# A fixed order for the seven products of the up projection, and weights of two early pairs made earlier

## The chip, the cores and the metric

The kernel runs on one core of one Trainium2 chip. The metric is device time in microseconds. The core has five engines with queues of their own that run in order: TensorE (PE, matmuls into PSUM), VectorE (DVE), ScalarE (ACT), GpSimd (POOL) and SyncE (SP, which issues most transfers).

## The reference

One layer of a decoder trunk over 1,024 tokens of width 1,024, in fp32: three mixers and an output projection, cross-attention over 256 memory tokens, and a gated MLP, each with a residual, and an RMSNorm at the end. The change lies at the end of the cross-attention and in the MLP:

```python
x = x + memory_cross_attention(h, rms_norm(mem, norm_mem_g[l]), ...)
h = rms_norm(x, norm_ffn_g[l])
x = x + conv_gated_ffn(h, ffn_w_up[l], ffn_conv_w[l], ffn_conv_b[l], ffn_w_down[l])
...
def conv_gated_ffn(h, w_up, conv_w, conv_b, w_down):
    u, v = jnp.split(h @ w_up, 2, axis=-1)
    u = lax.conv_general_dilated(u, conv_w[:, None, :], ...) + conv_b   # causal, width 3
    return (jax.nn.silu(u) * v) @ w_down
```

The hidden width of u and of v is 22 blocks of 128.

## The kernel before

Every fp32 product is made of three matmuls on rounded parts: each operand is split into a high part (`hi`, a ScalarE copy) and the rest (`lo`, a subtraction on VectorE or GpSimd), and hi x hi, hi x lo and lo x hi are summed in PSUM.

**Last attention product.** `tokmajor` multiplies the softmax by the prepared value weights (`vo_dram`), for two halves of tokens (0 to 3, 4 to 7, in blocks of 128) and two halves of columns, with four weight pieces each. A piece is loaded by SP (L137) into one of two `raw` buffers, cast to `whi` by ScalarE (L140), and `wlo` is made on VectorE (L143). `last` takes each finished block: residual sum (L1263), store of x2 (L1266, SP), norm (L1112 to L1115), and then the operands of the MLP, transposed on TensorE (L1254) and split (L1257, L1258).

**Up projection.** u and v of one block of hidden columns (a pair) are made with seven products in place of eight, as in Strassen's scheme over two halves of tokens and two halves of depth. The token operands are B11, B21 (tokens 0 to 3), T1, T2, T4 and later T3, B22 (with tokens 4 to 7). The weight operands are blocks of the raw weights (`t_up`) or sums of them made on GpSimd (`left`, L1308), each split into a `wf` tile (L1315 ScalarE, L1316 VectorE and GpSimd in turn). Each of the seven is twelve matmuls of 128x512 (`prod`, L1323). Raw weights lie in the two `raw` buffers and in residual rows that have come free. `ahead(f)` makes the B11 and B21 products of the first six pairs early and stores them in DRAM; `pair(f)` makes the others, for 22 pairs. Products go to PSUM tiles `ps_a` (B11, then B21), `ps_b2` (T2) and `ps_cd`, one tile of two halves c and d:

```python
cd = self.dps.tile([P, 1024], F32, tag="d", name="ps_cd")
c, d = cd[:, 0:512], cd[:, 512:1024]
...
self.prod(c, next(forms), X["T3"], True, True)
V.tensor_tensor(out=u3, in0=c, in1=u2, op=ALU.add)
self.prod(d, next(forms), X["T1"], True, True)
V.tensor_tensor(out=vt[:, 512:1024], in0=d, in1=u3, op=ALU.add)
```

T4 then adds to c and B22 to d, each read once more by VectorE (L1392, L1394). ScalarE and VectorE make the convolution and the gate from u (`y`, L1396 to L1400), and y goes to DRAM.

**Down projection.** `ffn_down` loads y and the weights again, splits both (`wd`, L1446 and L1447; `ap`, L1449 and L1450) and sums over 22 blocks in eight PSUM banks (`ps_dn`, L1436).

**Order.** The program is written in the order of the code; a scheduler then orders the instructions of each engine by its own estimate of times, and puts in the waits between engines. So products of neighbouring pairs are interleaved on TensorE.

Of the kernel before, what the change touches and what calls it, by code (L numbers as in the profile page):

```python
# [12 lines left out]
F32 = mybir.dt.float32  # L13
# [4 lines left out]
ALU = mybir.AluOpType  # L18
# [3 lines left out]
P = 128  # L22
S = 1024
DM = 1024
NK = 8
# [71 lines left out]
class K:  # L97
# [1098 lines left out]
    def trunk(self, mT, qk_dram, vo_dram, x2_dram, bp):  # L1196

        nc, tc, I = self.nc, self.tc, self.I
        V, A, G, T = nc.vector, nc.scalar, nc.gpsimd, nc.tensor

        xr = []
        for i in range(8):
            xr.append(self.res.tile([P, DM], F32, tag=f"r{i}", name="xr"))
            nc.sync.dma_start(out=xr[i], in_=I["x"][0, P * i:P * i + P, :])

        def resid(nm, g, T2):
            def f(c, i, o):
                xs = xr[i][:, 512 * c:512 * c + 512]
                V.tensor_tensor(out=xs, in0=o, in1=xs, op=ALU.add)
                if c == 1:  # L1210
                    xn = bp.tile([P, DM], F32, tag="xn", name="xn", bufs=2)
                    self.norm_g(bp, xr[i], g, xn)
                    self.to_T(xn, T2, i)
            return f

        h2 = self.halves("h2T")
        g2 = self.gain(bp, I["norm_xa_g"])
        self.tokmajor(I["t_out"], mT, resid("xa", g2, h2))
        pT = self.halves("pT")

        def soft(c, i, o):

            nm, z = (self.tiny.tile([P, 2], F32, tag=t, name=t, bufs=3) for t in ("s_nm", "s_z"))
            V.tensor_reduce(out=nm, in_=o.rearrange("p (h n) -> p h n", n=256), op=ALU.max, axis=AX.X)
            G.tensor_scalar(out=nm, in0=nm, scalar1=-1.0, scalar2=None, op0=ALU.mult)
            p_ = bp.tile([P, DM], F32, tag="xn", name="s_p", bufs=2)
            for j in range(2):
                js = slice(256 * j, 256 * j + 256)
                A.activation(out=p_[:, js], in_=o[:, js], func=AF.Exp, bias=nm[:, j:j + 1], accum_out=z[:, j:j + 1])
            V.reciprocal(out=z, in_=z)  # L1230
            ps = self.mps.tile([P, 512], F32, tag="m", name="ps_pT")
            for j in range(2):
                js = slice(256 * j, 256 * j + 256)
                G.tensor_scalar(out=p_[:, js], in0=p_[:, js], scalar1=z[:, j:j + 1], scalar2=None, op0=ALU.mult)
                for n in (2 * j, 2 * j + 1):
                    T.transpose(ps[:, P * n:P * n + P], p_[:, P * n:P * n + P], self.ident)
            p3 = ps.rearrange("p (k t) -> p k t", t=P)
            ts = slice(P * (i % 4), P * (i % 4) + P)
            hi, lo = (blk(pT[a][i // 4], c)[:, :, ts] for a in range(2))
            A.copy(out=hi, in_=p3)  # L1240
            V.tensor_tensor(out=lo, in0=p3, in1=hi.bitcast(F32), op=ALU.subtract)

        self.tokmajor(qk_dram, h2, soft)
        g3 = self.gain(bp, I["norm_ffn_g"])
        X, xk, held = {}, [], []

        def form(n, x, i):

            if n not in X:
                X[n] = [self.quad(f"{n}{p}") for p in ("hi", "lo")]  # L1250
            ts = slice(P * (i % 4), P * (i % 4) + P)
            ps = self.mps.tile([P, 512], F32, tag="m", name="ps_T")
            for j in range(4):
                T.transpose(ps[:, P * j:P * j + P], x[:, P * j:P * j + P], self.ident)  # L1254
            p3 = ps.rearrange("p (k t) -> p k t", t=P)
            hi, lo = (x[:, :, ts] for x in X[n])
            A.copy(out=hi, in_=p3)  # L1257
            V.tensor_tensor(out=lo, in0=p3, in1=hi.bitcast(F32), op=ALU.subtract)  # L1258

        def last(c, i, o):  # L1260

            xs = xr[i][:, 512 * c:512 * c + 512]
            V.tensor_tensor(out=xs, in0=o, in1=xs, op=ALU.add)  # L1263
            if c == 0:
                return
            nc.sync.dma_start(out=x2_dram[i], in_=xr[i])  # L1266
            if i % 2 == 0 and i < 4:
                xk.append(self.quad("xk", F32, (P, 2, DM)))
            xn = xk[i // 2][:, i % 2, :] if i < 4 else self.res.tile([P, DM], F32, tag=f"r{i - 4}", name="xn")
            self.norm_g(bp, xr[i], g3, xn)  # L1270
            x1, x2 = xn[:, 0:512], xn[:, 512:1024]
            if i < 4:
                form("B11", x1, i)
                form("B21", x2, i)
                return
            k = xk[i // 2 - 2]
            t1, t4 = k[:, i % 2, 0:512], k[:, i % 2, 512:1024]
            t2 = bp.tile([P, DM], F32, tag="xn", name="t2", bufs=2)[:, 0:512]
            V.tensor_tensor(out=t1, in0=x1, in1=t1, op=ALU.subtract)
            V.tensor_tensor(out=t2, in0=x2, in1=t1, op=ALU.subtract)  # L1280
            G.tensor_tensor(out=t4, in0=t4, in1=t2, op=ALU.subtract)
            G.tensor_tensor(out=x1, in0=x2, in1=x1, op=ALU.subtract)
            for n, x in (("T2", t2), ("T1", t1), ("T4", t4)):
                form(n, x, i)
            held.append((i, x1, x2))

        self.tokmajor(vo_dram, pT, last)
        for n in range(2):
            for i, *x in held:
                form(("T3", "B22")[n], x[n], i)  # L1290
        return X

    def left(self, r1, r2, which, sp):

        nc = self.nc
        V, A, G = nc.vector, nc.scalar, nc.gpsimd
        q = {f"A{n}{k + 1}": r[:, 4 * k:4 * k + 4, :] for n, r in ((1, r1), (2, r2)) if r is not None for k in range(2)}
        sums = {"S1": ("A21", "A22", ALU.add), "S2": ("S1", "A11", ALU.subtract), "S3": ("A11", "A21", ALU.subtract),  # L1300
                "S4": ("A12", "S2", ALU.subtract)}

        def get(n):
            if n not in q:
                a, b, op = sums[n]
                a, b = get(a), get(b)
                q[n] = sp.tile([P, 4, P], F32, tag=n, name=n, bufs=2 if n in ("S1", "S2") else 1)
                G.tensor_tensor(out=q[n], in0=a, in1=b, op=op)  # L1308
            return q[n]

        for n in which:
            x = get(n)
            self.nform = getattr(self, "nform", 0) + 1
            f = self.wp.tile([P, 2, 4, P], F32R, tag=("whi", "wlo")[self.nform % 2], name="wf")
            A.copy(out=f[:, 0], in_=x)  # L1315
            (V if self.nform % 2 else G).tensor_tensor(out=f[:, 1], in0=x, in1=f[:, 0].bitcast(F32), op=ALU.subtract)  # L1316
            yield f

    def prod(self, ps, f, x, start, stop):
        n = 0  # L1320
        for k in range(4):
            for a, b in ((0, 0), (0, 1), (1, 0)):
                self.nc.tensor.matmul(ps, lhsT=f[:, a, k, :], rhs=x[b][:, k, :], start=(start and n == 0), stop=(stop and n == 11),  # L1323
                                      skip_group_check=not start)
                n += 1

    def ffn_up(self, X, act, part, spill):

        nc, tc, I = self.nc, self.tc, self.I
        V, A, G, T = nc.vector, nc.scalar, nc.gpsimd, nc.tensor  # L1330
        with tc.tile_pool(name="up", bufs=1) as sp:
# [20 lines left out]
                    self.dps.tile([P, 1024], F32, tag="d", name="ps_a")[:, 0:512]  # L1352

            def ahead(f):
                forms, a = self.left(load(f, 4), None, ("A11", "A12"), sp), bank(f)
                self.prod(a, next(forms), X["B11"], True, True)
                nc.sync.dma_start(out=part[0, f], in_=copy("s1", a))
                yield
                self.prod(a, next(forms), X["B21"], False, True)
                c = spill.tile([P, 512], F32, tag="acr", name="c11")  # L1360
                A.copy(out=c, in_=a)
                nc.sync.dma_start(out=part[1, f], in_=c)
                yield
# [53 lines left out]
    def ffn_down(self, act, x2_dram, out, spill):  # L1417
        nc, tc, I = self.nc, self.tc, self.I
        V, A, G, T = nc.vector, nc.scalar, nc.gpsimd, nc.tensor
        with tc.tile_pool(name="down", bufs=1) as sp:  # L1420
# [3 lines left out]
            for tg in range(2):  # L1424
# [15 lines left out]
                for f in range(NFF):  # L1440
# [12 lines left out]
                            xr.append(self.res.tile([P, DM], F32, tag=f"r{(0, 1, 6, 7)[j]}", name="xr"))  # L1453
                            nc.sync.dma_start(out=xr[j], in_=x2_dram[4 * tg + j])
                    if f < NFF - tail:
                        for j in range(4):
                            step(f, j, (w[:, 0], w[:, 1]), a)
                    else:
                        held.append((f, (w[:, 0], w[:, 1]), a))
                for j in range(4):  # L1460
# [11 lines left out]
def program(tc, I, O, ctx):  # L1472
    nc = tc.nc
# [36 lines left out]
    with ExitStack() as c2:  # L1510
# [1 line left out]
        b.w2 = c2.enter_context(tc.tile_pool(name="w2", bufs=2))  # L1512
        bp = c2.enter_context(tc.tile_pool(name="trunk", bufs=1))
        b.lo_dve = 1
        X = b.trunk(mT, qk, vo, x2, bp)
        b.lo_dve = 2
    b.tps = ctx.enter_context(tc.tile_pool(name="tps", bufs=2, space=PSUM))
    part = dr.tile([2, 6, P, 512], F32, name="part_dram")
    spill = ctx.enter_context(tc.tile_pool(name="spill", bufs=4))
    b.ffn_up(X, act, part, spill)  # L1520
    b.ffn_down(act, x2, O["out"], spill)


# [27 lines left out]
```

## Time and profile before

| | us |
|---|---|
| median of 3 runs (lowest to highest) | 2444.51 (2444.17 to 2449.09) |
| profiled execution | 2446.41 |
| its span | 2444.5 |
| TensorE busy in the span | 2341.5 |
| VectorE, ScalarE, GpSimd busy | 1272.8, 885.0, 687.1 |

Times in the views count from the start of the span. A busy time of TensorE sums rows whose ends are modelled, since matmuls overlap; where it stands still is seen by idle times and by how many matmuls a stretch holds. The up projection's products lie between about 1720 and 2203, the down projection's between 2181 and 2436.

### The profile page before, as it was taken

How to read it: one execution, taken by the hardware profiler on the slowest of the kernel's cores; microseconds unless marked ns; L12 is line 12 of the kernel's file. 1: busy time of each engine (PE TensorE's matmuls, PEld its weight loads, DVE VectorE, ACT ScalarE, POOL GpSimd, SP SyncE). 2: the span in 40 equal slices, each digit the busy share in tenths (PEclk: the TensorE clock that was granted, in tenths of full speed). 3: DMA queues.
4: the chain of work that ended last, by engine and by line, in shares of the span. 5: the costliest groups of instructions: out<-in, count | busy, mean ns of one | idle time of the engine just before them, and what ended most of it. 6: DMA issues, size and time to landing. Idle time of an engine off the chain costs nothing. (4 is left out here: it accounts for less than half of the span.)

```text
span 2444.5 us, 34713 instructions
## 1 busy us (share of the span) xinstructions
PE 2341.5 (96%) x14120; PEld 1911.2 (78%) x14120; DVE 1272.8 (52%) x1937; ACT 885.0 (36%) x1350; POOL 687.1 (28%) x558
## 2 busy tenths in 40 slices
PE   7999989999999999999999999999889999989998
PEld 7987768676778887878878778888667888878887
DVE  6446465747425547464554464545545555564322
ACT  7542213231315335343541233443333433443321
POOL 1011011110112323333231530240465555553210
PEclk9999999999999999999999999999999999999999
DMA  8644213131212111111113662223443222236531
GB/s 304 227 164 129 83 57 96 57 96 40 96 54 74 61 52 35 46 41 60 36 61 119 204 211 88 94 88 128 147 151 105 89 78 79 92 134 234 164 138 48
DMA packets 101183, 260.35 MB, mean 107 GB/s; under 512 B 26144, under 2 KB 30880, under 8 KB 101024
## 3 DMA queue, kind: packets, MB, share of 16 engines
q1 hardware_dynamic: 99584, 254.06, 31.5%
q0 software_dynamic: 1008, 3.67, 0.4%
q8 instruction: 111, 1.82, 0.3%
q14 instruction: 48, 0.39, 0.1%
q10 hardware_dynamic: 432, 0.41, 0.0%
HBM read 197.28 MB, written 60.82 MB: 106 GB/s over the span
## 5 line engine op out<-in xcount | busy, mean ns | idle before, releaser
L155 PE MATMUL ps_d<-hThi,whi 128*128 128x512 f32 x1056 | 425.8, 404 | 2.3 <-DVE Ktt L261 1.9
L157 PE MATMUL ps_d<-hTlo,whi 128*128 128x512 f32 x1056 | 424.1, 402 | 0.0
L159 PE MATMUL ps_d<-hThi,wlo 128*128 128x512 f32 x1056 | 424.1, 402 | 0.0
L140 ACT CAST whi<-raw 128x1024 fp32r<-128x1024 f32 (+1 forms) x170 | 166.9, 988 | 331.1 <-PE ps_d L157 156.5
L1436 PE MATMUL ps_dn<-wd,ap 128*128 128x512 f32 x1056 | 241.7, 391 | 7.1 <-DVE ap L1450 6.3
L1436 PEld LDWEIGHTS ps_dn<-wd,ap 128*128 128x128 f32 x1056 | 199.0, 189 | 49.2 <-DVE ap L1450 6.7
L155 PEld LDWEIGHTS ps_d<-hThi,whi 128*128 128x128 f32 x1056 | 199.9, 189 | 44.8 <-issue 3.2
L157 PEld LDWEIGHTS ps_d<-hTlo,whi 128*128 128x128 f32 x1056 | 199.9, 189 | 43.1 <-issue 4.6
L159 PEld LDWEIGHTS ps_d<-hThi,wlo 128*128 128x128 f32 x1056 | 199.7, 189 | 42.8 <-issue 4.2
L143 DVE TENSOR_TENSOR wlo<-raw,whi 128x1024 fp32r<-128x1024 f32 (+1 forms) x125 | 157.8, 1270 | 135.7 <-ACT whi L140 135.7
L143 POOL TENSOR_TENSOR wlo<-raw,whi 128x1024 fp32r<-128x1024 f32 (+1 forms) x45 | 95.8, 2130 | 449.6 <-ACT whi L140 387.2
L1315 ACT CAST wf<-S 128x512 fp32r<-128x512 f32 x88 | 54.6, 622 | 160.7 <-PE ps_cd L1323 73.6
L1450 DVE TENSOR_TENSOR ap<-acr,ap 128x512 fp32r<-128x512 f32 x44 | 37.4, 851 | 134.0 <-ACT ap L1449 134.0
L1113 POOL TENSOR_SCALAR ms<-ms 128x1 f32<-128x1 f32 x33 | 10.8, 329 | 268.3 <-ACT xn L1112 146.0
L1447 POOL TENSOR_TENSOR wd<-wdr,wd 128x1024 fp32r<-128x1024 f32 x22 | 54.8, 2492 | 107.5 <-ACT wd L1446 107.5
L155 PE MATMUL ps_d<-ohi,whi 128*128 128x512 f32 x192 | 75.7, 398 | 7.2 <-ACT ohi L1164 5.8
L1316 POOL TENSOR_TENSOR wf<-S,wf 128x512 fp32r<-128x512 f32 x44 | 62.7, 1424 | 63.9 <-ACT wf L1315 63.9
L1449 ACT CAST ap<-acr 128x512 fp32r<-128x512 f32 x44 | 27.3, 622 | 143.2 <-PE ps_dn L1436 121.9
L745 DVE CUSTOM_DVE_ANT_0 a_p<-ps_s,a_bias 128x512 f32<-128x512 f32 (+3 forms) x96 | 51.7, 552 | 50.3 <-PE ps_s L743 45.0
L755 ACT ACTIVATE a_p<-a_p,a_nm 128x128 f32<-128x128 f32 (+7 forms) x64 | 49.1, 769 | 76.1 <-POOL a_nm L751 58.6
L157 PE MATMUL ps_d<-olo,whi 128*128 128x512 f32 x192 | 76.1, 396 | 0.6 <-DVE olo L1165 0.5
L159 PE MATMUL ps_d<-ohi,wlo 128*128 128x512 f32 x192 | 75.9, 395 | 0.1
(423 smaller groups left out, 5286.3 us busy)
## 6 DMA issues: line engine op xcount, KB each, us to landing
raw<-t_in SPq DMA_DIRECT2D x66, 512.0 KB, 3.6
raw<-t_up SPq DMA_DIRECT2D x50, 512.0 KB, 3.5
wdr<-ffn_w_down SPq DMA_DIRECT2D x44, 512.0 KB, 4.0
th_dram<-th SPq DMA_DIRECT2D x24, 512.0 KB, 2.8
mth<-th_dram SPq DMA_DIRECT2D x24, 512.0 KB, 3.6
acr<-act_dram SPq DMA_DIRECT2D x44, 256.0 KB, 2.7
act_dram<-y SPq DMA_DIRECT2D x20, 512.0 KB, 2.6
raw<-t_kv SPq DMA_DIRECT2D x16, 512.0 KB, 4.9
```

Of the source, the lines that this page charges most:

```text
L140: nc.scalar.copy(out=hi, in_=raw)
L143: eng.tensor_tensor(out=lo, in0=raw, in1=hi.bitcast(F32), op=ALU.subtract)
L155: nc.tensor.matmul(o, lhsT=hi[:, k, :], rhs=xhi(k, h), start=(k == 0), stop=False)
L157: nc.tensor.matmul(o, lhsT=hi[:, k, :], rhs=xlo(k, h), start=False, stop=False)
L159: nc.tensor.matmul(o, lhsT=lo[:, k, :], rhs=xhi(k, h), start=False, stop=(k == nk - 1))
L745: V.tensor_tensor_reduce(out=p_[:, a:b], in0=ps[:, 0:b - a], in1=bias[:, 1024 - n + a:1024 - n + b], op0=ALU.add, op1=ALU.max, scale=1.0, ...
L755: A.activation(out=pr[c][:, 0:n], in_=pr[c][:, 0:n], func=AF.Exp, bias=nm[:, c:c + 1], accum_out=Z[:, c:c + 1])
L1315: A.copy(out=f[:, 0], in_=x)
L1316: (V if self.nform % 2 else G).tensor_tensor(out=f[:, 1], in0=x, in1=f[:, 0].bitcast(F32), op=ALU.subtract)
L1436: T.matmul(ps[j][c], lhsT=a[:, p, P * j:P * j + P], rhs=w[q][:, 512 * c:512 * c + 512], start=(f == 0 and n == 0), stop=(f == NFF - 1 and ...
L1447: (V if f % 2 else G).tensor_tensor(out=w[:, 1], in0=wr, in1=w[:, 0].bitcast(F32), op=ALU.subtract)
L1450: V.tensor_tensor(out=a[:, 1], in0=ar, in1=a[:, 0].bitcast(F32), op=ALU.subtract)
```

## The change

Three things change. `prod` chains every product behind the one written before it (`issue_after`), and the first step of the down projection behind the last product, so TensorE gets them in the order of the code. In the last attention product, once tokens 0 to 3 are normed, the raw weights of the pairs 0 and 1 are loaded and split (`early`), for the B11 and B21 products that `ahead` begins with. The eight residual rows are given out in another order, and the normed rows of tokens 4 to 7 with them.

```diff
-            xr.append(self.res.tile([P, DM], F32, tag=f"r{i}", name="xr"))
+            xr.append(self.res.tile([P, DM], F32, tag=f"r{(0, 1, 6, 7, 2, 3, 4, 5)[i]}", name="xr"))
...
-            xn = xk[i // 2][:, i % 2, :] if i < 4 else self.res.tile([P, DM], F32, tag=f"r{i - 4}", name="xn")
+            xn = xk[i // 2][:, i % 2, :] if i < 4 else self.res.tile([P, DM], F32, tag=f"r{(0, 1, 6, 7)[i - 4]}", name="xn")
...
             if i < 4:
                 form("B11", x1, i)
                 form("B21", x2, i)
+                if i == 3:
+                    for f in range(2):
+                        r = self.wp.tile([P, NK, P], F32, tag="raw", name="raw")
+                        nc.sync.dma_start(out=r, in_=I["t_up"][f])
+                        w = self.quad("wf0", shape=(P, 2, 2, 4, P))
+                        for n in range(2):
+                            self.split(w[:, n], r[:, 4 * n:4 * n + 4, :], V)
+                        early.append(iter((w[:, 0], w[:, 1])))
                 return
...
-            A.copy(out=f[:, 0], in_=x)
-            (V if self.nform % 2 else G).tensor_tensor(out=f[:, 1], in0=x, in1=f[:, 0].bitcast(F32), op=ALU.subtract)
+            self.split(f, x, V if self.nform % 2 else G)
             yield f
 
+    def split(self, f, x, eng):
+
+        self.nc.scalar.copy(out=f[:, 0], in_=x)
+        eng.tensor_tensor(out=f[:, 1], in0=x, in1=f[:, 0].bitcast(F32), op=ALU.subtract)
+
     def prod(self, ps, f, x, start, stop):
...
+        with self.tc.issue_after(self.behind) if self.behind is not None else ExitStack():
+            n = 0
+            for k in range(4):
+                for a, b in ((0, 0), (0, 1), (1, 0)):
+                    i = self.nc.tensor.matmul(ps, lhsT=f[:, a, k, :], rhs=x[b][:, k, :], start=(start and n == 0),
+                                              stop=(stop and n == 11), skip_group_check=not start)
+                    n += 1
+        self.behind = i.ins
+
+    behind = None
...
-                forms, a = self.left(load(f, 4), None, ("A11", "A12"), sp), bank(f)
+                forms, a = early[f] if f < len(early) else self.left(load(f, 4), None, ("A11", "A12"), sp), bank(f)
...
-                        for j in range(4):
-                            step(f, j, (w[:, 0], w[:, 1]), a)
+                        with tc.issue_after(self.behind) if tg == f == 0 else ExitStack():
+                            for j in range(4):
+                                step(f, j, (w[:, 0], w[:, 1]), a)
```

What it does to the order of SP's queue, from the loads of the output projection's weights on, before (`x_dram<-xr` are the stores of x2):

```order
L137 DMA raw<-t_out 128x1024 x12
L137 DMA raw<-qk_dram 128x1024 x16
L137 DMA raw<-vo_dram 128x1024 x13
L1266 DMA x_dram<-xr 128x1024 x4
L137 DMA raw<-vo_dram 128x1024 x3
L1342 DMA raw<-t_up 128x1024 x3
```

and now:

```order
L137 DMA raw<-t_out 128x1024 x12
L137 DMA raw<-qk_dram 128x1024 x16
L137 DMA raw<-vo_dram 128x1024 x8
L1278 DMA raw<-t_up 128x1024 x2
L1266 DMA x_dram<-xr 128x1024 x4
L137 DMA raw<-vo_dram 128x1024 x8
L1360 DMA raw<-t_up 128x1024 x3
```

Two loads of up weights come after eight value weights, and five of the value weights that stood ahead of the four stores now stand behind them.

TensorE's order inside the pairs, from the end of a T4 product to the B22 product of the same pair (`ps_cd_15274`; `ps_a_15392` and `ps_cd_15412` belong to the next pair), before; a row's brackets name the engines that it waits for:

```order
L1323 MATMUL ps_cd_15274<-T4hi_14163,wf_15347 128x512
L1323 MATMUL ps_a_15392<-B11hi_13798,wf_15393 128x512 [waits Pool_49]
L1323 MATMUL ps_a_15392<-B11hi_13798,wf_15393 128x512
L1323 MATMUL ps_a_15392<-B11lo_13799,wf_15393 128x512
L1323 MATMUL ps_a_15392<-B11hi_13798,wf_15393 128x512 x2
L1323 MATMUL ps_a_15392<-B11lo_13799,wf_15393 128x512
L1323 MATMUL ps_a_15392<-B11hi_13798,wf_15393 128x512 x2
L1323 MATMUL ps_a_15392<-B11lo_13799,wf_15393 128x512
L1323 MATMUL ps_a_15392<-B11hi_13798,wf_15393 128x512
L1323 MATMUL ps_cd_15412<-T3hi_14295,wf_15437 128x512 [waits Activation_49]
L1323 MATMUL ps_cd_15412<-T3lo_14296,wf_15437 128x512
L1323 MATMUL ps_cd_15274<-B22hi_14325,wf_15365 128x512 [waits DVE_49]
```

and now, the same place of a pair:

```order
L1338 MATMUL ps_cd_15272<-T4hi_14177,wf_15345 128x512 x2
L1338 MATMUL ps_cd_15272<-T4lo_14178,wf_15345 128x512
L1338 MATMUL ps_cd_15272<-T4hi_14177,wf_15345 128x512
L1338 MATMUL ps_cd_15272<-B22hi_14339,wf_15363 128x512 [waits DVE_49,Activation_49]
L1338 MATMUL ps_cd_15272<-B22lo_14340,wf_15363 128x512
L1338 MATMUL ps_cd_15272<-B22hi_14339,wf_15363 128x512 x2
```

Products of the next pair stood between T4 and B22; now B22 follows T4 at once. Its wait for VectorE is the same in both: VectorE's read of T4's half of the tile.

At the end of the up projection, TensorE had, before:

```order
L1436 MATMUL ps_dn<-wd,ap 128x512 x15
L1323 MATMUL ps_cd<-T4hi,wf 128x512
L1323 MATMUL ps_cd<-T4lo,wf 128x512
L1323 MATMUL ps_cd<-T4hi,wf 128x512 x2
L1323 MATMUL ps_cd<-T4lo,wf 128x512
L1323 MATMUL ps_cd<-T4hi,wf 128x512 x2
L1323 MATMUL ps_cd<-T4lo,wf 128x512
L1323 MATMUL ps_cd<-T4hi,wf 128x512 x2
L1323 MATMUL ps_cd<-T4lo,wf 128x512
L1323 MATMUL ps_cd<-T4hi,wf 128x512
L1436 MATMUL ps_dn<-wd,ap 128x512 x21
```

and now:

```order
L1338 MATMUL ps_cd<-B22hi,wf 128x512 x2
L1338 MATMUL ps_cd<-B22lo,wf 128x512
L1338 MATMUL ps_cd<-B22hi,wf 128x512 x2
L1338 MATMUL ps_cd<-B22lo,wf 128x512
L1338 MATMUL ps_cd<-B22hi,wf 128x512
L1454 MATMUL ps_dn<-wd,ap 128x512 x1056
```

The first 36 matmuls of the down projection stood ahead of and between the last pair's T4 and B22; now all 1,056 stand behind B22.

## Rows read from the trace of the kernel before

**Rows 1.** The page, part 1: busy time, share and instructions by engine.

```profile
PE 2341.5 (96%) x14120; PEld 1911.2 (78%) x14120; DVE 1272.8 (52%) x1937; ACT 885.0 (36%) x1350; POOL 687.1 (28%) x558
```

**Rows 2.** Stretches: length, busy PE, PEld, DVE, ACT, POOL, clock, DMA share, GB/s.

```profile
1660.00:1720.00 60.00, 60.00 (x282) 50.03 (x281) 27.27 (x32) 19.37 (x28) 4.47 (x9) 1.00 0.34 115
1720.00:1770.00 50.00, 41.21 (x190) 32.66 (x190) 30.46 (x35) 22.03 (x42) 25.30 (x22) 0.90 0.48 164
1770.00:1905.00 135.00, 122.06 (x519) 95.39 (x518) 68.06 (x78) 45.67 (x65) 81.68 (x58) 0.99 0.37 126
1905.00:2180.00 275.00, 275.00 (x1209) 225.90 (x1207) 161.45 (x168) 115.58 (x166) 151.71 (x104) 1.00 0.27 88
2180.00:2205.00 25.00, 17.89 (x66) 13.93 (x65) 18.12 (x13) 9.12 (x13) 10.86 (x6) 0.86 0.61 203
2205.00:2436.00 231.00, 230.99 (x1019) 190.97 (x1018) 74.68 (x81) 64.06 (x89) 46.66 (x32) 1.00 0.43 144
```

**Rows 3.** Stretches, L1254 alone: length, PE, PEld, clock, DMA share, GB/s.

```profile
1720.00:1770.00 50.00, 10.06 (x64) 7.75 (x64) 0.90 0.48 164
1770.00:1905.00 135.00, 2.40 (x16) 1.99 (x16) 0.99 0.37 126
```

**Rows 4.** Waits of PE, 1720 to 1905: us in sum, times, longest.

```profile
PE ps_T L1254 <- DVE t L1280: 3.7, 1, 3.7
PE ps_cd L1323 <- ACT wf L1315: 3.1, 4, 0.9
```

**Rows 5.** Waits of PE, 1905 to 2206.

```profile
PE ps_dn L1436 <- DVE ap L1450: 6.3, 1, 6.3
```

**Rows 6.** Timeline around 2203: start, length, engine, line, operation, idle time before.

```profile
2203.33 0.39 PE L1323 MATMUL ps_cd<-B22hi,wf 128*128 128x512 f32 x1
2203.75 0.69 DVE L1394 TENSOR_TENSOR u<-ps_cd,u 128x512 f32<-128x512 f32 x1 [0.48 <-PE ps_cd L1323]
2204.50 0.96 PE L1436 MATMUL ps_dn<-wd,ap 128*128 128x512 f32 x3 [0.79 <-DVE u L1394]
```

**Rows 7.** Groups, 1905 to 2180: sum and mean ns | idle before.

```profile
L1316 DVE TENSOR_TENSOR wf<-S,wf 128x512 fp32r<-128x512 f32 x28 | 32.6, 1164 | 14.7 <-ACT wf L1315 14.4
L1400 DVE TENSOR_TENSOR y<-y,vt 128x1024 f32<-128x1024 f32 x14 | 25.0, 1787 | 7.9 <-ACT y L1399 7.9
L1397 DVE SCALAR_TENSOR_TENSOR y<-u,par,y 128x1024 f32<-128x1024 f32 x15 | 21.4, 1423 | 4.6 <-ACT y L1396 4.1
L1396 ACT ACTIVATE y<-u,par 128x1024 f32<-128x1024 f32 x15 | 18.7, 1247 | 2.6 <-DVE u L1394 1.3
L1394 DVE TENSOR_TENSOR u<-ps_cd,u 128x512 f32<-128x512 f32 x15 | 10.4, 692 | 42.6 <-PE ps_cd L1323 42.6
```

**Rows 8.** DMA issues, 1640 to 1700: KB each, median us to landing.

```profile
raw<-vo_dram SPq DMA_DIRECT2D x11, 512.0 KB, 3.4
```

**Rows 9.** Timeline, last attention product; the last row from PE alone.

```profile
1672.52 1.28 DVE L1263 TENSOR_TENSOR xr<-ps_tm,xr 128x512 f32<-128x512 f32 x2
1675.36 1.28 DVE L1115 SCALAR_TENSOR_TENSOR xk<-xr,rs,gain 128x1024 f32<-128x1024 f32 x1 [1.55 <-POOL rs L1114]
1680.88 1.04 PE L1254 MATMUL ps_T<-ident,xk 128*128 128x128 f32 x8
1681.67 0.48 PE L1099 MATMUL ps_tm<-whi,pThi 128*128 128x512 f32 x1
```

**Rows 10.** Stretches of PE alone: length, busy PE, clock, DMA share, GB/s.

```profile
1739.40:1744.30 4.90, 4.90 (x14) 0.52 0.23 92
1804.00:1870.00 66.00, 58.44 (x243) 1.00 0.38 130
```

**Rows 11.** Timeline, transposes behind the last attention product.

```profile
1746.49 0.66 PE L1254 MATMUL ps_T<-ident,t 128*128 128x128 f32 x4 [1.09 <-DVE T1lo L1258]
1748.64 0.63 PE L1254 MATMUL ps_T<-ident,xk 128*128 128x128 f32 x4 [0.90 <-DVE T2lo L1258]
```

More of the change, by code (lines that the diff above doesn't have):

```diff
@@ L1244, in trunk @@
         g3 = self.gain(bp, I["norm_ffn_g"])
-        X, xk, held = {}, [], []
+        X, xk, held, early = {}, [], [], []
         def form(n, x, i):
@@ L1290, in trunk @@
                 form(("T3", "B22")[n], x[n], i)
-        return X
+        return X, early
     def left(self, r1, r2, which, sp):
         nc = self.nc
-        V, A, G = nc.vector, nc.scalar, nc.gpsimd
+        G = nc.gpsimd
+        V = nc.vector
         q = {f"A{n}{k + 1}": r[:, 4 * k:4 * k + 4, :] for n, r in ((1, r1), (2, r2)) if r is not None for k in range(2)}
@@ L1314, in left, with ffn_up @@
             f = self.wp.tile([P, 2, 4, P], F32R, tag=("whi", "wlo")[self.nform % 2], name="wf")
-            A.copy(out=f[:, 0], in_=x)
-            (V if self.nform % 2 else G).tensor_tensor(out=f[:, 1], in0=x, in1=f[:, 0].bitcast(F32), op=ALU.subtract)
+            self.split(f, x, V if self.nform % 2 else G)
             yield f
+    def split(self, f, x, eng):
+        self.nc.scalar.copy(out=f[:, 0], in_=x)
+        eng.tensor_tensor(out=f[:, 1], in0=x, in1=f[:, 0].bitcast(F32), op=ALU.subtract)
     def prod(self, ps, f, x, start, stop):
[L1320 to L1327, printed above, removed]
+        with self.tc.issue_after(self.behind) if self.behind is not None else ExitStack():
[7 more added lines that the diff above has]
+    behind = None
+    def ffn_up(self, X, early, act, part, spill):
         nc, tc, I = self.nc, self.tc, self.I
@@ L1514, in program @@
         b.lo_dve = 1
-        X = b.trunk(mT, qk, vo, x2, bp)
+        X, early = b.trunk(mT, qk, vo, x2, bp)
         b.lo_dve = 2
@@ L1519, in program @@
     spill = ctx.enter_context(tc.tile_pool(name="spill", bufs=4))
-    b.ffn_up(X, act, part, spill)
+    b.ffn_up(X, early, act, part, spill)
     b.ffn_down(act, x2, O["out"], spill)
```

## The prediction, made before the changed kernel was run

> **What bounds the kernel now.** I read the page's busy shares first, then the table of stretches, then the waits of TensorE, then single stalls in the timeline. TensorE is busy 96% of the span [rows 1], so only time that it loses can be won or added. Its pace when nothing stops it is in the down projection: 1,019 matmuls in 231.00 us, 0.2267 us each [rows 2]; eight transposes take 1681.67 - 1680.88 = 0.79 us, 0.10 each [rows 9]. Priced so, each stretch shows its loss:
> - 1720 to 1770 (end of the trunk, first products of the up projection): 190 operations, 64 of them transposes [rows 2, 3]: 126 x 0.2267 + 6.4 = 35.0 of 50 us, 15.0 lost.
> - 1770 to 1905 (first pairs): 519, 16 of them transposes: 115.6 of 135, 19.4 lost.
> - 1905 to 2180 (the other pairs): 1,209: 274.1 of 275, 0.9 lost.
> - 2180 to 2205 (into the down projection): 66: 15.0 of 25, 10.0 lost.
> Together 45.4 us. The waits name the causes: split weights that come late from ScalarE (for ps_cd four times, up to 0.9 us), 3.7 us behind a form that VectorE makes [rows 4], and 6.3 us behind the split activation of the down projection [rows 5], whose first 15 matmuls stand ahead of the last pair's T4 product. After long idleness the clock falls: from 1739.40 to 1744.30 it was 0.52 of full speed, so at the lower of its two levels, 1.2 GHz, and 14 operations took 4.9 us where 14 x 0.2267 = 3.2 would do, or less if some are transposes: a fall costs about 2 us [rows 10]. Between 1804 and 1870 TensorE was busy for 58.44 of 66 us, idle for 7.6 in short stops, and the clock stayed at 1.00, 2.4 GHz [rows 10].
>
> **What the change gives back.** Chaining the products puts them on TensorE in the order in which their split weights are made, and the two first pairs' weights come early. I let the 19.4 us of the first pairs go but for 2 us (the raw weights of pair 0 still arrive after the early products). The down projection's first matmuls no longer stand ahead of T4 and B22, so the 10.0 falls to about 1 us (0 to 4). In the transition the 24 matmuls of B11 run at once (5.4 us) but then the 48 transposes of T2, T1 and T4 have nothing between them, and two PSUM banks: eight go every 1748.64 - 1746.49 = 2.15 us [rows 11], 48 take 12.9, so the last is done 18.3 us after the attention product; 18.3 - 5.4 - 4.8 = 8.1 lost and one fall of the clock, 10 us (8 to 14) in place of 15.0. The stretch 1905 to 2180 keeps its 0.9 us besides what follows.
>
> **What it adds, first: a stop behind PSUM reads.** T3 and T1 write the two halves of one PSUM tile, ps_cd, and T4 and B22 write them again. The wait of the first T1 matmul is on VectorE's read of T3's half; T4 waits for the read of T1's, B22 for that of T4's. Before, the scheduler put other products between (T2, B11 or B21 of a neighbour), so VectorE's 0.69 us passed unseen. In a fixed order nothing is between: T3 runs straight into T1 and T4 into B22 in every pair, and T1 into T4 too in the six pairs that have no B21 of their own. That is 16 x 2 + 6 x 3 = 50 stops. The trace has one such stop, with VectorE free: the last up matmul starts at 2203.33, the read at 2203.75 (0.69 us), the next matmul at 2204.50 [rows 6]. The read began 0.42 us behind the last matmul's start. That is 1.17 us from start to start instead of 0.23: 0.94 lost. 50 x 0.94 = 47 us. It can't be less where the read follows the last matmul and the next follows the read. It is more where VectorE is held up in its queue: the read of T3 stands behind the product y (1.79 us on average) and a split (1.16) [rows 7]. From the end of a pair: its last read ends at 0.9, ScalarE's first pass on y (1.25 [rows 7]) at 2.1, VectorE's two passes (1.42 each [rows 7]) at 5.0, the read of T2 at 6.3, y's product at 8.1, a split at 9.3 if one stands there; T3 would be read from 8.4. So nothing to 0.9 us more, half of it in the middle, in about 11 of the pairs: 5 us. I take 52, with 47 and 70 (1.4 a stop) as ends.
>
> **Second: the two early weight loads.** SP's queue is in order. Before, 13 loads of vo weights stood ahead of the four x2 stores; now 8, then the two t_up loads, then the stores, then the rest. So the weights for tokens 4 to 7, which TensorE multiplied before while it waited for the norms, are not there. Their load also needs one of two raw buffers, both held by t_up until the splits are done, and those stand on VectorE behind the norm of the fourth token. Worked out from before: the first two tokens' residual sums begin at 1672.5 [rows 9], the other two tokens need 12 matmuls more (2.7 us), so the block ends at about 1675.2. The first normed rows come at 1675.4 + 1.3 = 1676.7 [rows 9]; three more at 1.25 each (a ScalarE pass of that width [rows 7]) make it 1680.4, four splits of some 0.8 us (0.69 is VectorE's shortest row of that width [rows 6], 1.16 the mean [rows 7]) 1683.6; the load lands 3.4 us later [rows 8], at 1687.0; ScalarE's pass on it takes up to 1.25, so matmuls again at about 1688.2. Of these 13.0 us TensorE fills 2.4 with 24 transposes: 10.6 lost, and a fall of the clock: 13 us (9 to 17). Before, it was busy for all of the 60 us from 1660 to 1720 [rows 2]. The place change of residual rows only lets raw loads find rows free; I cost it at nothing, since a pair's two loads (3.4 us each) lie beside 16 us and more of products.
>
> **The sum.** After: 13 + 10 + 2 + 52 + 1 + 0.9 = 78.9 us lost, before 45.4: 33.5 us more. The profiled execution took 2446.41 us (span 2444.5), so 2479.9. The median lies 1.9 us below it: **2478 us**.
>
> **The clock in the pairs.** The stops between 1804 and 1870 came about as often as the 50 would come and left the clock at 1.00 [rows 10], so the sum has no falls for them. The Trainium skill (TensorE: Matmul & The Clock Gate, section on psum-queue depth-cycling) warns of just this pattern: short idle times between groups of matmuls that go from one PSUM bank to the next made the clock swing between its levels in another kernel. By that rule falls would come on top of the 52 us; the trace has not agreed so far. What such falls would cost is in rival 3.
>
> **Rivals.**
> 1. The reads don't show (another product covers them, or the two halves don't wait for each other). The losses are 13 + 10 + 2 + 1 + 0.9 = 26.9, 18.5 us less than before: 2426 us, faster. It decides when more than 33.5 of the 52 us are covered, that is, when a stop costs under 0.37 us. For it: the stretch 1905 to 2180 shows such waits covered to 0.9 us. Against: that order had other products between, and the new one has none. Chance 0.07.
> 2. The early loads don't hold up the vo product, because its weights arrive while the norms run. Then 13 becomes 0: 2465 us. For it: the queue has only four stores more to pass. Against: the buffers are held until the splits. Chance 0.13.
> 3. VectorE is late for nearly every stop, or the clock falls. VectorE's product y takes 1.79 us on average [rows 7] where a norm of the same width took 1.28 [rows 9], so its operations are at times stretched; late by 1 us in each of 22 pairs is 22 us: 2500. A fall of the clock (2 us) in every second pair gives 22 as well. For it: VectorE's queue is in order. Against: the clock from 1804 to 1870 [rows 10]. Chance 0.10, of which the clock 0.03.
> My forecast has 0.70, with 2464 to 2496 as its own range.
>
> **Range and chances.** The ends of the terms: 9 + 8 + 47 and 0 elsewhere is 64.9 with the 0.9, 2464; all high is 17 + 14 + 4 + 70 + 4 + 0.9 = 109.9, 2509. Leaving out rival 1 and the outermost part of 2 and 3, the range is 2456 to 2500. A change under 0.2% (5 us) could not be told from none; only something between rival 1 and 2 lies there, 0.03. Slower 0.90, faster 0.07.
>
> **What would show it.** Right: waits of TensorE's ps_cd on VectorE's u and vt, some 50 of them with about 0.8 us of idle time each; some 100 matmuls fewer in the stretch 1905 to 2180 (13 pairs of about 21 us, each with two stops of 0.94); an idle stretch of about 10 us near 1676 that ends in the vo weights; no stop of TensorE behind ap at the start of the down projection. Wrong: TensorE at 0.2267 us a matmul through the pairs, or no gap in the vo product.

## The result and the profile after

The changed kernel takes 2516.72 us in the median of 4 runs (2512.34 to 2517.66) against 2446.48 for the kernel before in the same comparison (4 runs, 2444.17 to 2449.09): a ratio of 1.0281, with a 95% interval of 1.0265 to 1.0296. It is slower, as forecast, but by 70 us where the forecast said 33.5; the range ended at 2500. The profiled execution has a span of 2515.0 us, 70.5 longer than before.

The table of stretches answers to [rows 2]; its columns are the same. The trunk's last product now ends near 1741, the up projection near 2267, so the stretches are cut there.

```profile
1675.00:1700.00 25.00, 16.93 (x70) 12.89 (x69) 17.30 (x21) 13.07 (x22) 4.27 (x8) 0.73 0.45 168
1740.00:1798.00 58.00, 48.62 (x224) 39.18 (x224) 28.83 (x35) 22.98 (x43) 26.67 (x23) 0.85 0.44 151
1798.00:1905.00 107.00, 89.41 (x373) 68.10 (x372) 57.63 (x63) 34.23 (x46) 61.87 (x44) 1.00 0.37 118
1905.00:2180.00 275.00, 241.38 (x1032) 192.65 (x1031) 140.41 (x141) 92.78 (x136) 142.96 (x92) 0.99 0.21 69
2180.00:2260.00 80.00, 69.19 (x287) 54.93 (x286) 38.44 (x43) 28.99 (x42) 34.55 (x23) 0.96 0.27 90
2260.00:2275.00 15.00, 12.68 (x56) 10.21 (x55) 12.98 (x10) 9.40 (x12) 7.39 (x4) 1.00 0.88 299
```

The same table for the transposes alone, where there are any (columns as in [rows 3]):

```profile
1675.00:1700.00 25.00, 5.35 (x28) 4.48 (x29) 0.73 0.45 168
1740.00:1798.00 58.00, 15.22 (x80) 11.87 (x80) 0.85 0.44 151
```

Priced as in the prediction (0.2267 us a matmul, 0.10 a transpose) the losses are 12.7 us in the attention product, 17.4 in the transition, and 22.4, 41.0, 14.9 and 2.3 in the pairs and the step into the down projection. The stretch 1905 to 2180 held 1,209 matmuls before and holds 1,032 now. Together, with 0.5 us between 1700 and 1740, that is 111.2 us, 65.8 more than the 45.4 of before. Of the 4.7 us that are left of the 70.5, 4.0 lie ahead of the change: a cast of the value weights that began at 1640.21 us before begins at 1644.17 now, with the same instructions up to there. In the traces of the other runs the same cast begins between 1637.93 and 1645.16, and at 1638.56 in one that has the whole change ahead of it (the run with y's product moved), so the change didn't put them there.

The waits of TensorE between 1660 and 2275, as in [rows 4] us in sum, times and the longest:

```profile
PE ps_cd L1338 <- DVE u L1403: 37.8, 22, 3.4
PE ps_cd L1338 <- DVE vt L1410: 20.7, 22, 2.3
PE ps_T L1254 <- DVE T2lo L1258: 6.9, 2, 6.0
PE ps_T L1254 <- DVE B11lo L1258: 6.8, 2, 5.1
PE ps_cd L1338 <- DVE vt L1405: 5.3, 6, 0.9
```

The 50 stops are there to the number: 22 behind the read of T3 (L1403), 22 behind that of T4 (L1410), 6 behind that of T1 (L1405). Of the waits for split weights, as in [rows 4], one of 0.4 us is left, and the wait for ap of [rows 5] is gone.

### The profile page after: what moved, and what is told of

It is laid out like the page before. It is cut to its first block, busy times and chain, and to the rows that moved or that the text cites. A ratio compares the mean times of both kernels' runs of the same rounds, so it can differ in the third digit from the quotient of the medians.

```text
span 2515.0 us, 34811 instructions
## 1 busy us (share of the span) xinstructions
PE 2357.4 (94%) x14120; PEld 1914.9 (76%) x14120; DVE 1281.0 (51%) x1939; ACT 885.1 (35%) x1350; POOL 695.9 (28%) x556
## 4 chain that ended last, share of the span: by engine, by line
PE 70%; DVE 13%; issue 7%; ACT 4%; DMA 4%; POOL 2%; SPq 0%; DVEq 0%; POOLq 0%; ACTq 0%
PE ps_tm L1099 10%; PE ps_d L159 9%; PE ps_d L157 9%; PE ps_d L155 9%; PE ps_cd L1338 8%; PE ps_dn L1454 6%; PE ps_a L1338 4%; PE ps_l L942 1%; PE ps_b L1338 1%; PE ps_c L279 1%; DVE tmpa L453 1%; DVE wlo L143 1%; DVE tha L455 1%; PE ps_Y L279 1%; PE ps_qk L1056 1%
## 5 line engine op out<-in xcount | busy, mean ns | idle before, releaser
L1338 PE MATMUL ps_cd<-T1hi,wf 128*128 128x512 f32 x176 | 62.8, 419 | 37.8 <-DVE u L1403 37.8
L1330 POOL TENSOR_TENSOR wf<-S,wf 128x512 fp32r<-128x512 f32 x44 | 56.6, 1287 | 118.9 <-ACT wf L1329 118.8
L1338 PE MATMUL ps_cd<-B22hi,wf 128*128 128x512 f32 x176 | 59.7, 400 | 20.7 <-DVE vt L1410 20.7
L1317 POOL TENSOR_TENSOR S<-raw 128x512 f32<-128x512 f32 x44 | 64.5, 1469 | 44.2 <-DVE wf L1330 38.5
```

Source lines behind the costliest of these rows:

```text
L1330: eng.tensor_tensor(out=f[:, 1], in0=x, in1=f[:, 0].bitcast(F32), op=ALU.subtract)
L1338: i = self.nc.tensor.matmul(ps, lhsT=f[:, a, k, :], rhs=x[b][:, k, :], start=(start and n == 0), stop=(stop and n == 11), skip_group_check ...
```

## The experiments

The runs were timed in groups, each beside the kernel before, whose median was 2446.48, 2447.97, 2447.06 and 2444.42 us in turn. Ratios are to the kernel before of the same group; a difference of two medians from different groups is sure to some 3 us only.

**Two PSUM tiles, the fixed order kept.**

```diff
-                cd = self.dps.tile([P, 1024], F32, tag="d", name="ps_cd")
-                c, d = cd[:, 0:512], cd[:, 512:1024]
+                c = self.dps.tile([P, 1024], F32, tag="d", name="ps_c")[:, 0:512]
+                d = self.dps.tile([P, 1024], F32, tag="d", name="ps_d2")[:, 512:1024]
```

Each of the two tiles is as large as the old one and uses one half; they take the two buffers that the pool had for ps_cd.

> The changed kernel with the halves c and d of ps_cd as two PSUM tiles, in the same fixed order. Theory (50 stops behind VectorE's reads of ps_cd cost about 80 us, 1.2 to 2.1 each): the stops go, about 2437 us (2430 to 2450), and TensorE's waits for u (L1403) and vt fall from 64 us to under 8. Rival (in a fixed order the split weights come too late, and the reads only hide it): waits for wf take their place, 2490 to 2517 us.

Measured: 2437.44 us (2436.01 to 2440.45), a ratio of 0.9958 to the kernel before (0.9943 to 0.9973). Of TensorE's waits from 1798 to 2275 one is left:

```profile
PE ps_dn L1454 <- DVE u L1412: 2.8, 1, 2.8
```

The stops cost 2516.7 - 2437.4 = 79.3 us, and no wait for weights takes their place: the rival falls.

**The chain between products taken out of the changed kernel.**

```diff
-        with self.tc.issue_after(self.behind) if self.behind is not None else ExitStack():
+        with ExitStack():
```

> The changed kernel without the chain between products; the early weights, the rows and the place of the down projection stay. Theory: the stops go with the fixed order, the 19 us of the first pairs come back, the 13 us in the attention product stay: 2446 to 2460 us. Rival (the early weights and rows carry most of the loss): above 2490 us.

Measured: 2454.25 us (2448.96 to 2456.30), ratio 1.0024 (1.0010 to 1.0037). With the scheduler's order 62 us come back; the waits for split weights return with it (3.9 us for T2, 3.1 for ps_cd), and the 6.8 us behind B11lo stay. So early weights and rows carry little of the loss.

**No early weights.**

```diff
-                    for f in range(2):
+                    for f in range(0):
```

> The changed kernel without the two early pairs' weights. Theory: the 12.7 us lost in the attention product between 1675 and 1700 go, and some of it comes back in the transition: 2504 to 2512 us. Rival (the weights of that product would be late anyway): 2515 to 2519 us.

Measured: 2504.0 us (2498.56 to 2504.93), ratio 1.0224 (1.0208 to 1.0239), 12.7 less than the changed kernel. The stop in the attention product belongs to the early weights.

**Two PSUM tiles and no early weights.** Both edits above.

> Two PSUM tiles and no early weights, in the fixed order. Theory: both losses go, 2516.7 - 80 - 13 = 2424 us (2418 to 2436), faster than before. Rival (split weights too late in a fixed order): above 2480 us.

Measured: 2424.73 us (2423.30 to 2429.37), ratio 0.9902 (0.9886 to 0.9919). The two losses add up; without both the kernel is faster than before.

**Why a stop behind T3 costs more: y's product moved.** In the changed kernel, VectorE's product y of a pair and the store behind it are issued behind the read of T3 of the next pair.

```diff
-                V.tensor_tensor(out=u3, in0=c, in1=u2, op=ALU.add)
+                r3 = V.tensor_tensor(out=u3, in0=c, in1=u2, op=ALU.add)
+                if fin is not None:
+                    with tc.issue_after(r3.ins):
+                        fin()
...
-                V.tensor_tensor(out=y, in0=y, in1=vt, op=ALU.mult)
-                (nc.gpsimd if f >= NFF - 2 else nc.sync).dma_start(out=act[f], in_=y)
+                def fin():
+                    V.tensor_tensor(out=y, in0=y, in1=vt, op=ALU.mult)
+                    (nc.gpsimd if f >= NFF - 2 else nc.sync).dma_start(out=act[f], in_=y)
+                return fin
```

> The changed kernel with VectorE's product y of a pair placed behind the read of T3 of the next pair, instead of ahead of it. Theory (that read is late because VectorE's queue has y's product ahead of it): TensorE's waits for u3 fall from 37.8 to about 20 us, 2496 to 2504 us. Rival (VectorE is late anyway, its operations being stretched while GpSimd works): 2512 to 2518 us.

Measured: 2497.5 us (2494.75 to 2499.83), ratio 1.0203 (1.0180 to 1.0225), 19.2 less than the changed kernel. TensorE's waits from 1798 to 2275:

```profile
PE ps_cd L1338 <- DVE vt L1413: 22.8, 22, 4.4
PE ps_cd L1338 <- DVE u L1403: 22.7, 22, 2.3
PE ps_cd L1338 <- DVE vt L1408: 4.4, 5, 0.9
```

The waits behind T3 fall from 37.8 to 22.7 us, 1.03 each, the others hardly move: with y's product no longer ahead of it, the read is hardly late. The rival's number falls.

**B21 between T3 and T1.** From the seventh pair on, in the fixed order.

```diff
-                forms = self.left(*rs, ("S2", "S3", "S1", "A22", "S4") if f < ne else ("A11", "S2", "S3", "S1", "A12", "A22", "S4"), sp)
+                forms = self.left(*rs, ("S2", "S3", "S1", "A22", "S4") if f < ne else ("A11", "S2", "S3", "A12", "S1", "A22", "S4"), sp)
...
                 self.prod(c, next(forms), X["T3"], True, True)
                 V.tensor_tensor(out=u3, in0=c, in1=u2, op=ALU.add)
+                if f >= ne:
+                    self.prod(a, next(forms), X["B21"], False, True)
+                    A.copy(out=u[:, 2:514], in_=a)
                 self.prod(d, next(forms), X["T1"], True, True)
                 V.tensor_tensor(out=vt[:, 512:1024], in0=d, in1=u3, op=ALU.add)
-                if f >= ne:
-                    self.prod(a, next(forms), X["B21"], False, True)
-                    A.copy(out=u[:, 2:514], in_=a)
```

> The changed kernel with the B21 product of the pairs from the seventh on between T3 and T1 instead of between T1 and T4, in the same fixed order. As many stops (50), but those behind T3 are covered and those behind T1 are open. Theory (a stop costs 0.94 us with VectorE free, and only the one behind T3 more): 16 stops of about 2.1 us become 16 of 0.94, 2494 to 2503 us. Rival (all stops are alike in mean): 2513 to 2520 us.

Measured: 2502.28 us (2496.82 to 2506.06), ratio 1.0217 (1.0197 to 1.0238), 14.4 less than the changed kernel, just inside the theory's range. The waits behind T3 are 6.7 us in 7 stops, those behind T1 19.3 in 21, those behind T4 28.4 in 22. One of the last is new and takes 10.03 us: in the last pair, VectorE splits operands of the down projection ahead of the read. It hides some 9 us of the gain; the reads behind T1 and the other ones behind T4 take 0.9 us each, so a stop costs by what VectorE has to do, not by its place alone.

**The down projection's first step alone.** The kernel before, with this edit and `self.behind` set in `prod`:

```diff
+                        with tc.issue_after(self.behind) if tg == f == 0 else ExitStack():
+                            for j in range(4):
+                                step(f, j, (w[:, 0], w[:, 1]), a)
```

> The kernel before, with only the first step of the down projection chained behind the last product. Theory (15 of its matmuls ahead of T4 cost 10 us with the clock's fall): 8 us less than before, 2437 to 2441 us. Rival (the split activation is as late in any order): 2444 to 2449 us.

Measured: 2449.01 us (2445.55 to 2454.42), ratio 1.0002 (0.9991 to 1.0013): nothing. The theory falls for this step. The rival's number holds, though TensorE doesn't wait for the split activation any more. VectorE's rows ahead of T4's first matmul (the last row is TensorE's):

```profile
2176.29 3.37 DVE L1398 SCALAR_TENSOR_TENSOR y<-u,par,y 128x1024 f32<-128x1024 f32 x1
2179.70 2.17 DVE L1399 SCALAR_TENSOR_TENSOR y<-u,par,y 128x1024 f32<-128x1024 f32 x1
2181.79 3.37 DVE L1448 TENSOR_TENSOR wd<-wdr,wd 128x1024 fp32r<-128x1024 f32 x1
2185.09 2.82 DVE L1451 TENSOR_TENSOR ap<-acr,ap 128x512 fp32r<-128x512 f32 x1
2187.83 0.68 DVE L1388 TENSOR_TENSOR vt<-ps_cd,u 128x512 f32<-128x512 f32 x1
2188.66 0.76 PE L1323 MATMUL ps_cd<-T4hi,wf 128*128 128x512 f32 x1 [8.79 <-DVE vt L1388]
```

The splits of the down projection (wd, ap) stand on VectorE ahead of the read that T4 waits for. The wait of 6.3 us [rows 5] became one of 8.8: what TensorE's queue no longer waits for now stands ahead of it in VectorE's.

**Two PSUM tiles in the kernel before, the scheduler's own order.** The first edit alone.

> The kernel before, with the halves c and d as two PSUM tiles and the scheduler's own order. Theory (the scheduler had covered the reads; the pairs from 1905 on lost 0.9 us): 2443 to 2449 us. Rival (the single tile forced the interleaving that made the weights late for the first pairs, 19 us): 2425 to 2436 us.

Measured: 2422.14 us (2420.08 to 2423.72), ratio 0.9891 (0.9873 to 0.9909). The theory falls; the rival's way holds, and the gain is larger than its range. The stretches, columns as in [rows 2]:

```profile
1720.00:1770.00 50.00, 41.42 (x196) 32.78 (x196) 30.53 (x35) 22.08 (x42) 25.29 (x22) 0.93 0.50 169
1770.00:1905.00 135.00, 132.03 (x589) 108.77 (x588) 84.16 (x91) 54.01 (x77) 100.32 (x64) 1.00 0.39 136
```

From 1770 to 1905 it runs 589 operations where there were 519 [rows 2], 70 x 0.2267 = 16 us won in this stretch alone. TensorE's waits for split weights of the up projection from 1720 to 1905 fall from 13.0 to 3.3 us. So the single tile is what made the first pairs wait. Most of the rest of the 25 us lies in the step into the down projection, where 3.8 us are lost from 2150 to 2205 (226 operations) and 10.0 were before.

**The early weights in a buffer of their own.** The changed kernel, with

```diff
+                    rq = self.quad("rawe", F32, (P, 2, NK, P))
                     for f in range(2):
-                        r = self.wp.tile([P, NK, P], F32, tag="raw", name="raw")
+                        r = rq[:, f]
```

> The changed kernel with the two early pairs' raw weights in a buffer of their own instead of the two raw buffers. Theory (the weights for tokens 4 to 7 wait for those buffers, 12.7 us): SP's queue again has 13 loads ahead of the stores, TensorE doesn't stop between 1675 and 1700, 2502 to 2509 us. Rival (VectorE, busy with the four splits ahead of the operands of token block 1, holds up the transposes): 2512 to 2518 us.

Measured: 2502.6 us (2500.87 to 2504.11), ratio 1.0239 (1.0225 to 1.0253), 14.1 less than the changed kernel. Its SP queue:

```profile
1643.06 30.46 SPq L137 DMA_DIRECT2D raw<-vo_dram  x8
1673.80 8.14 SPq L1266 DMA_DIRECT2D x_dram<-xr  x4
1681.98 1.22 SPq L1279 DMA_DIRECT2D rawe<-t_up  x2
1684.82 8.58 SPq L137 DMA_DIRECT2D raw<-vo_dram  x3
```

Its order has 13 loads of value weights ahead of the stores again, and TensorE runs 124 operations from 1675 to 1700 without a gap, where the changed kernel ran 70. But the two loads of up weights now come behind the stores, and VectorE's four splits of them begin at 1688.29 only, behind the operands of token block 1. So the run takes away the buffers' hold and the splits' place together: the rival's condition isn't in it, and the rival stays untested by it.

**The same buffer and two tiles: every part of the change kept, though the early weights come as late as in the run above.**

> The same buffer and two PSUM tiles, in the fixed order: every part of the change is kept, both losses are taken away. Theory: 2437.4 - 13 = 2424 us (2419 to 2429). Whether the early weights are worth anything is read against the version without them, 2424.7: a gain would show as 2421 or less.

Measured: 2422.67 us (2420.21 to 2424.13), ratio 0.9909 (0.9896 to 0.9923). Against 2424.73 without the early weights and 2422.14 for the two tiles alone in the scheduler's order, nothing that can be told apart.

**Two tiles and the down projection's first step, in the scheduler's order.**

> The kernel before with two PSUM tiles and the first step of the down projection behind the last product, in the scheduler's order otherwise. If what the down projection's matmuls cost ahead of T4 only moves into VectorE's queue: 2420 to 2426 us, as with two tiles alone (2422.1). If the two tiles relieve that queue: 2415 to 2419 us.

Measured: 2421.53 us (2418.22 to 2425.81), ratio 0.9908 (0.9895 to 0.9922). Again no gain over two tiles alone: TensorE waits 2.3 us for VectorE at that place in either run, so little was left to win.

**The residual rows alone.**

```diff
-            xr.append(self.res.tile([P, DM], F32, tag=f"r{i}", name="xr"))
+            xr.append(self.res.tile([P, DM], F32, tag=f"r{(0, 1, 6, 7, 2, 3, 4, 5)[i]}", name="xr"))
...
-            xn = xk[i // 2][:, i % 2, :] if i < 4 else self.res.tile([P, DM], F32, tag=f"r{i - 4}", name="xn")
+            xn = xk[i // 2][:, i % 2, :] if i < 4 else self.res.tile([P, DM], F32, tag=f"r{(0, 1, 6, 7)[i - 4]}", name="xn")
```

> The kernel before with only the residual rows in the new order. By every theory no difference: 2445 to 2450 us. If the raw loads of the first pairs had waited for rows, 5 us or more would be won.

Measured: 2447.6 us (2442.72 to 2451.21), ratio 1.0011 (1.0002 to 1.0020): under 0.2%, as costed.

## Why the prediction was wrong in size and right in kind

Of the 36.9 us by which the profiled execution (2516.75) went over the forecast for it (2479.9), the pairs hold 23.4 (78.3 us lost, where the forecast had 2 + 52 + 0.9), the transition 7.4 and the step into the down projection 1.3; 4.7 are the ones that lie outside the stretches.

**The stops behind PSUM reads: right in mechanism and number, 79 us and not 52.** The step that failed is the price of VectorE's queue ahead of T3's read, "half of it in the middle, in about 11 of the pairs: 5 us", and with it the end of 70. Followed from matmul to matmul in the trace, the term has these parts:

- A stop with VectorE free loses 1.03 or 1.04 us from start to start (one is shown below), and the matmul behind it another 0.08: 56 us for 50 stops, not 47. The one stop in [rows 6] had shown 0.94.
- T3's reads are late. Behind T4 and T1 a stop took 0.94 and 0.88 us of idle time on average, behind T3 37.8 / 22 = 1.72. What goes beyond 0.88 behind T3 is 18.4 us in sum, not 5. In the first six pairs the idle time is 0.88 to 1.20 us, in the next fourteen 2.25 (once 2.20) and 1.61 in turn, in the last two 0.88 and 3.45.
- The clock fell twice, some 4 us (below), and one stop behind T4, in the last pair, took 1.4 us more than the others.

Together that is 80 us, beside the 79.3 between the runs with one tile and with two. One stop behind T3, VectorE, ScalarE's first pass and TensorE from the end of a pair on, with a GpSimd operation beside them:

```profile
2061.37 0.69 DVE L1412 TENSOR_TENSOR u<-ps_cd,u 128x512 f32<-128x512 f32 x1 [3.15 <-PE ps_cd L1338]
2062.14 1.24 ACT L1414 ACTIVATE y<-u,par 128x1024 f32<-128x1024 f32 x1 [0.15 <-DVE u L1412]
2063.42 1.75 DVE L1415 SCALAR_TENSOR_TENSOR y<-u,par,y 128x1024 f32<-128x1024 f32 x1 [0.71 <-ACT y L1414]
2064.16 2.15 POOL L1317 TENSOR_TENSOR S<-S,raw 128x512 f32<-128x512 f32 x1
2065.20 2.20 DVE L1416 SCALAR_TENSOR_TENSOR y<-u,par,y 128x1024 f32<-128x1024 f32 x1
2067.32 0.68 DVE L1401 TENSOR_TENSOR u<-ps_b,s 128x512 f32<-128x512 f32 x1
2068.53 1.23 DVE L1418 TENSOR_TENSOR y<-y,vt 128x1024 f32<-128x1024 f32 x1 [0.53 <-ACT y L1417]
2069.67 0.69 DVE L1330 TENSOR_TENSOR wf<-raw,wf 128x512 fp32r<-128x512 f32 x1
2070.27 0.69 DVE L1403 TENSOR_TENSOR u<-ps_cd,u 128x512 f32<-128x512 f32 x1
2071.10 0.47 PE L1338 MATMUL ps_cd<-T1hi,wf 128*128 128x512 f32 x1 [1.61 <-DVE u L1403]
```

The reader sees the chain of the prediction link by link: the passes on y take 1.75 and 2.20 us beside GpSimd's sum and not 1.42, the product of y then waits for ScalarE, and T3's read comes behind all of it. The product belongs to the pair before, the split behind it to a later product: TensorE needs neither at this point. In every second of these fourteen pairs a split stands further ahead, between the passes and T2's read, and it and the product take longer:

```profile
2044.17 1.78 DVE L1330 TENSOR_TENSOR wf<-raw,wf 128x512 fp32r<-128x512 f32 x1
2046.48 1.81 DVE L1418 TENSOR_TENSOR y<-y,vt 128x1024 f32<-128x1024 f32 x1
2049.04 0.47 PE L1338 MATMUL ps_cd<-T1hi,wf 128*128 128x512 f32 x1 [2.25 <-DVE u L1403]
```

The last pair but one has the same order on VectorE. But there GpSimd starts nothing between 2219.7 and 2223.9, each operation takes its short time, and the read isn't late:

```profile
2220.98 1.28 DVE L1416 SCALAR_TENSOR_TENSOR y<-u,par,y 128x1024 f32<-128x1024 f32 x1
2222.18 0.69 DVE L1330 TENSOR_TENSOR wf<-raw,wf 128x512 fp32r<-128x512 f32 x1
2223.66 1.22 DVE L1418 TENSOR_TENSOR y<-y,vt 128x1024 f32<-128x1024 f32 x1
2225.34 0.39 PE L1338 MATMUL ps_cd<-T3hi,wf 128*128 128x512 f32 x1
2225.76 0.69 DVE L1403 TENSOR_TENSOR u<-ps_cd,u 128x512 f32<-128x512 f32 x1 [0.89 <-PE ps_cd L1338]
2226.60 0.47 PE L1338 MATMUL ps_cd<-T1hi,wf 128*128 128x512 f32 x1 [0.88 <-DVE u L1403]
```

This is a stop with VectorE free, 2226.60 - 2225.34 = 1.26 us where 0.2267 would do. So it takes both to make the read late: y's product ahead of it, and the stretch. Moving the product won 19.2 us, which shows the first; for the second there is this one pair, and no run of its own. The prediction had named what stands in the queue and priced it with the mean durations of the old order. Its rival 3 had the lateness at 1 us in each of 22 pairs, 22 us, and a chance of 0.07: near the 18.4 that came, but it came together with the other misses.

**The clock: nearly as the row said.** The table above has 0.96 to 1.00 for the pairs, though the stops came two to three a pair. Seen closer, the clock fell to its lower level, 1.2 GHz, twice (columns as in [rows 10]):

```profile
2003.90:2007.40 3.50, 3.50 (x10) 0.51 0.55 174
2249.60:2256.60 7.00, 6.13 (x15) 0.51 0.92 331
```

The first fall comes behind a stop of 2.25 us like five others that left the clock at 1.00; the second begins within the stop of 3.45. The forecast had no falls in the pairs; at 0.2267 us a matmul and without the rest of that stop, these two cost some 4 us, an estimate. The longer falls came in the attention product, 0.73 from 1675 to 1700, and in the transition, 0.85, where single stops lasted 5.1 and 6.0 us. The Trainium skill (TensorE: Matmul & The Clock Gate, section "A second HAM failure mode: psum-queue depth-cycling") tells of a kernel whose clock swung between its levels because TensorE idled briefly and often between groups of matmuls. This trace agrees only that far: two falls in 50 stops, and 1.00 between them.

**The early loads: right in size, in part by luck.** Forecast 13 us; the trace shows 12.7 us, and the runs 12.7 (no early weights) and 14.1 (a buffer of their own), or 13.9 and 10.3 by their ratios. The parts were others than forecast: TensorE's idle rows from 1675 to 1700 are 8.0 us and not 10.6, and the lower clock took the rest, more than the 2 of one fall. The way there, in the changed kernel:

```profile
1676.23 4.83 SPq L1266 DMA_DIRECT2D x_dram<-xr  x4
1683.97 2.17 ACT L1329 CAST wf<-raw 128x512 fp32r<-128x512 f32 x4
1687.52 1.89 DVE L1330 TENSOR_TENSOR wf<-raw,wf 128x512 fp32r<-128x512 f32 x3
1688.23 1.52 SPq L137 DMA_DIRECT2D raw<-vo_dram  x2
1691.46 1.04 ACT L140 CAST whi<-raw 128x1024 fp32r<-128x1024 f32 x1 [4.34 <-DMA raw<-vo_dram]
```

The second of the four splits frees the first raw buffer at about 1688.2 (1687.52 + 0.68). At 1688.23 the value weights are asked for, and ScalarE's idle time of 4.34 us ends when they land; TensorE's matmuls go on at 1692.55. The transposes waited as well, 5.1 us for B11lo, behind the same splits on VectorE, but they were done at 1692.0. So both hold TensorE up, and the weights come last, as forecast; no run parts the two. The value weights were forecast to be asked for at 1683.6 and to be cast by 1688.2; both came some 4 us later, as does everything from 1640 on.

**The transition: 17.4 us and not 10.** The step had eight transposes every 2.15 us behind B11's matmuls, 12.9 us for 48. B11's matmuls began 1.2 us late, behind a residual sum, and the transposes took 18.8 us, from 1746.28 to 1765.12. They waited 5.96 us once, for T2lo, and went on at the lower clock. T2lo's other half was ready early: T2hi ended at 1746.91 + 0.59 = 1747.50, but VectorE made its low half at 1752.45 only, behind a norm and sums of later token blocks (two of them shown):

```profile
1746.91 0.59 ACT L1257 CAST T2hi<-ps_T 128x512 fp32r<-128x512 f32 x1 [4.75 <-PE ps_T L1254]
1748.57 2.28 DVE L1115 SCALAR_TENSOR_TENSOR xn<-xr,rs,gain 128x1024 f32<-128x1024 f32 x1
1750.77 1.75 DVE L1288 TENSOR_TENSOR t<-xn,xk 128x512 f32<-128x512 f32 x1
1752.45 0.68 DVE L1258 TENSOR_TENSOR T2lo<-ps_T,T2hi 128x512 fp32r<-128x512 f32 x1
1753.27 1.08 PE L1254 MATMUL ps_T<-ident,xk 128*128 128x128 f32 x4 [5.96 <-DVE T2lo L1258]
```

So both misses lie in VectorE's queue: in the pairs it was priced too short, and here the norm and the sums ahead of the awaited half were not in the sum at all. This one was not tried by a run of its own.

**What is given back: right in the changed kernel, its cause not.** The waits for split weights went, and the step into the down projection lost 2.3 us (forecast 1). But the chain of the down step alone won nothing, since the wait moved to VectorE's queue. And the 19 us of the first pairs need no fixed order: two tiles win them in the scheduler's own order. Why the single tile made the weights late there is only argued: with it the scheduler may have filled in products of neighbours whose weights came in another order than they were asked for.

**Rivals.** The first (2426 us) needed covered reads, or halves that don't wait for each other; in the run with two tiles they don't, and it took 2437, with the transition's 7 us in the difference. The second did not come about. Of the third, VectorE's lateness came and the clock hardly.

## What to carry to other kernels

When an order is fixed by hand, ask first what the scheduler's mixed order had been covering: here every read of an accumulator by another engine, at about 1.1 us or more apiece. Dependencies counted on one tile for two independent halves were cheaper to remove than to schedule around: splitting the PSUM tile won 25 us in the kernel before, and with it the fixed order cost nothing that shows any more. A wait taken from one in-order queue comes back if the awaited operation stands behind the same work in another; read what stands ahead of it there, and price that with the durations under load.

## What had not been expected of the hardware

VectorE's operations on two SBUF inputs stretched far more beside GpSimd than the mean of before showed: two passes on y took 1.75 and 2.20 us in one pair, and one took 3.37 at the end of the up projection (in the run with the down projection's first step alone), against 1.28 for an operation of that width alone. In the whole trace of the changed kernel, 97 of these 128x1024 fp32 operations have no GpSimd tensor operation beside them and took 1.21 to 1.29 us; of the 58 that have one, the longest took 3.44. Reads of PSUM kept to 0.68 or 0.69 us in all these rows.
